# Moving a hybrid block's mixer stage off GpSimd arithmetic: conditioning to TensorE, weight splits and state-space products to VectorE

## The chip, the cores and the metric

The kernel runs on one core of a Trainium2 chip. The metric is device time in microseconds of one launch, the median of several runs. The engines are TensorE (PE; its weight loads are listed as PEld), VectorE (DVE), ScalarE (ACT), GpSimd (POOL) and SyncE (SP). SP, ACT and POOL also issue DMAs, each in a queue of its own that works in order with the engine's other instructions.

## What is computed

A sequence of 512 tokens of width 1024 goes through one conditioned block and two further layers. Cut to what matters here:

```python
def first_block(x, c, w_ada, b_ada, w_in, ...):
    ada = silu(c) @ w_ada[0] + b_ada[0]              # 6 * 1024 values
    sh_m, sc_m, g_m, sh_f, sc_f, g_f = split(ada, 6)
    h = rms_norm(x) * (1 + sc_m) + sh_m
    proj = h @ w_in[0]                               # 1792 columns z, 512 columns u
    z = z + mu * (z_prev - z)
    mix = concat([rwkv7_time_mix(z, ...), s5_mix(u, ...)]) @ w_out[0]
    x = x + g_m * mix
    h = rms_norm(x) * (1 + sc_f) + sh_f
    x = x + g_f * ((silu(h @ w_gate) * (h @ w_up)) @ w_down)
    return rms_norm(x) * final_gain
# then second_block: two layers of latent attention, short convolution and
# sliding-window attention, each x + concat(...) @ w_out_2
```

`ada` is one row of 6144 values. The first 2048 (shift and scale of the first norm) are needed before the first product, `g_m` before the mixer's output is added, the rest before the FFN.

## The kernel before

Activations lie feature-major: 128 features by 512 tokens a tile, eight tiles for x. Each f32 weight tile is loaded raw, copied by ACT to a rounded high part (`whi`), and the rest `wlo = wraw - whi` is taken by DVE or POOL. A product is then three matmuls of type fp32r: hi by hi, hi by lo, lo by hi. This splitting is in `Weights.convert` and, for the first product, in `conv0`. The engine of the subtraction is an entry of the weight list: for the mixer `LOENG` (POOL), for FFN and layers `LWENG` (DVE for every fourth tile, POOL for the others).

The program is a set of threads (Python generators) that yield instructions. The class `Flow` fixes one order for each engine before the program runs: at each turn it takes the instruction that can start first by a rough cost (`Flow.cost`) plus a bias of the thread (`BIAS`). Engines then run that order strictly, so an instruction whose input is late holds up whatever stands behind it on its engine. `turn` gives the weight products of the mixer (`gemm_g`) their places as filler between other matmuls.

The mixer (`mixer`, from L1497) has these parts, in the order of time:

- `norm_g` loads x, forms the norm and, feature tile by feature tile, `h`. Tile k needs the conditioning values k (shift) and 8 + k (scale).
- `cond` and `condpe` make these 16 groups of 128 values. The weights come transposed, so that for 12 of them one DVE instruction multiplies a 128x1024 tile `wa` by silu(c) spread over all partitions (`cact`) and sums along the row. For the four in `ADAPE`, `condpe` multiplies on PE with the weights stationary and one moving column. `loada0` loads the tiles on SP's queue into three buffers.
- `load0`, `conv0` and `gemm0` are the first product: u and three of the fourteen z blocks (`Z3 = (12, 0, 4)`), weights loaded on SP's queue, their low parts on POOL.
- `Prepare` builds the state-space matrices from their parameters on DVE; its `products` are eight items of five instructions, of which `PREP` gives four inject items and one output item to POOL and three output items to DVE. `response` clears the matrix `toep` on POOL and fills it by way of DRAM.
- `S5` is the state-space branch, from the first product's end to about 230 us.
- `Mix` is the time mix, four pairs of heads one after another (`front_a`, `invert`, `front_b`, `solve`, `chain`, `norm`), from about 180 to 500 us. Between its small matmuls PE does the remaining z blocks, the gate and the output products, in the order of `JOBS`; their weights are loaded on POOL's queue (`LOADQ`).
- `ada_g` makes the other 32 groups of conditioning values during the time mix: a tile `wa` is loaded on ACT's queue (`ADAQ`), multiplied by `cact` on POOL, and summed along the row by an ACT instruction with an accumulator. Two buffers.
- `evac_c` sums squares for the FFN's norm, two of its sums on POOL (`TAILENG`).

The FFN and the two layers follow (`second`), from about 490 us on; POOL has work of theirs too.

Of the kernel before, what the change touches and what calls it, by code (L numbers as in the profile page):

```python
# [8 lines left out]
F32 = mybir.dt.float32  # L9
# [16 lines left out]
# ---------------------------------------------------------------- host layout  # L26
# [71 lines left out]
LOENG = lambda X: X.pool  # L98
Z3 = (12, 0, 4)
# [44 lines left out]
def pack(i):  # L144
# [12 lines left out]
    o["w3"] = np.concatenate([w_in[:, 128 * m:128 * m + 128] for m in Z3], 1).reshape(8, 128, 3, 128)  # L157
# [60 lines left out]
# ---------------------------------------------------------------- device  # L218
class Ctx:
    """Engine shorthands and the helpers that every part uses."""  # L220
# [49 lines left out]
    def wtile(self, src, *shape, full=False):  # L270
        """weights as hi + lo, exactly"""
# [17 lines left out]
    def gemm(self, ps, src, K, hi, lo):  # L289
        """ps[128 cols, 512 tok] = sum_k src[:, k].T @ (hi + lo)[:, k]"""  # L290
# [10 lines left out]
    def gemms(self, pss, srcs, K, hi, lo, col, cols):  # L301
        """several products of the same operand, side by side; and of the column col, in parts, to cols"""
# [75 lines left out]
class Flow:  # L378
    """Puts the instructions of several threads (generators) in one order per engine: at each turn the
    instruction that can start first, by a rough count of what each takes, and keeps that order."""  # L380

    DMA_RATE = 360e3  # bytes a microsecond
    # from the end of an instruction on one engine to the start of one that needs it on another
# [10 lines left out]
    # -- an instruction: function, arguments; the first argument (or out) is written, the rest read  # L394
# [30 lines left out]
    def cost(eng, fn, out, args, kw=None):  # L425
# [4 lines left out]
        if eng == "PE":  # L430
# [11 lines left out]
            return 4 * max(n, m) / 2400.0  # L442
# [48 lines left out]
    # -- the tensor engine's clock: full speed only after a window with enough columns streamed  # L491
# [15 lines left out]
    def turn(self, o, plan, bias):  # L507
        """when this instruction would have its turn; work that fills in comes as the clock needs it"""
# [60 lines left out]
    def run(self):  # L569
        while self.live:  # L570
# [18 lines left out]
            # what is over before the best can start goes first  # L589
# [16 lines left out]
class Ring:  # L606
    """room for a few tiles of one kind, which threads take and free"""
# [22 lines left out]
class Pairs:  # L630
    """a ring of hi and lo"""
# [865 lines left out]
def mixer(X, top, stop):  # L1497
# [81 lines left out]
    def cond(cT):  # L1579
# [1321 lines left out]
```

## Time and profile before

| what | value |
|---|---|
| median of three runs | 1649.7 us (1642.33 to 1653.17) |
| profiled execution, first to last instruction | 1651.5 us |
| mean granted TensorE clock | 0.958 |
| busy PE / DVE / ACT / POOL | 1528.3 / 930.6 / 679.6 / 657.2 us |
| instructions PE / DVE / ACT / POOL | 8564 / 1988 / 1368 / 546 |
| moved by DMA | 141.88 MB |

The span of the profiled execution lies within the three runs and 1.8 us above their median; no other time of that execution is shown. Busy time is the union of an engine's instructions. A matmul's record lasts longer than its distance from the next one, so a busy PE can still take more. f32 matmuls have two records each. The granted clock is a share of 2.4 GHz.

### The profile page before, as it was taken

How to read it: one execution, taken by the hardware profiler on the slowest of the kernel's cores; microseconds unless marked ns; L12 is line 12 of the kernel's file. 1: busy time of each engine (PE TensorE's matmuls, PEld its weight loads, DVE VectorE, ACT ScalarE, POOL GpSimd, SP SyncE). 2: the span in 40 equal slices, each digit the busy share in tenths (PEclk: the TensorE clock that was granted, in tenths of full speed). 3: DMA queues.
4: the chain of work that ended last, by engine and by line, in shares of the span. 5: the costliest groups of instructions: out<-in, count | busy, mean ns of one | idle time of the engine just before them, and what ended most of it. 6: DMA issues, size and time to landing. Idle time of an engine off the chain costs nothing.

```text
span 1651.5 us, 23242 instructions
## 1 busy us (share of the span) xinstructions
PE 1528.3 (93%) x8564; PEld 1176.8 (71%) x8564; DVE 930.6 (56%) x1988; ACT 679.6 (41%) x1368; POOL 657.2 (40%) x546
## 2 busy tenths in 40 slices
PE   4699888798987999999999999999999999999998
PEld 4576575566655888888888867776778866867776
DVE  7986677867687422222215473464774575364772
ACT  3332443334434333333333465364454365355351
POOL 4652054555444333333443454632225344633222
PEclk9999997887998999999999999999999999999999
DMA  5453042453312222323332311312112311221112
GB/s 180 152 95 75 22 125 87 119 171 99 110 64 70 83 96 96 100 98 90 99 96 71 95 58 52 102 52 64 58 52 84 92 53 63 79 75 58 58 46 95
DMA packets 98800, 141.88 MB, mean 86 GB/s; under 512 B 40944, under 2 KB 45936, under 8 KB 98672
## 3 DMA queue, kind: packets, MB, share of 16 engines
q1 hardware_dynamic: 89360, 111.55, 22.9%
q10 hardware_dynamic: 5904, 17.85, 3.4%
q0 software_dynamic: 3424, 11.01, 2.2%
q8 instruction: 67, 1.10, 0.3%
q14 instruction: 45, 0.37, 0.1%
HBM read 135.39 MB, written 4.98 MB: 85 GB/s over the span
## 4 chain that ended last, share of the span: by engine, by line
PE 74%; DVE 20%; ACT 4%; issue 2%; DMA 0%; ACTq 0%; POOL 0%; DVEq 0%; POOLq 0%
PE mm L255 53%; PE rp L255 11%; PE O L255 3%; PE rp L524 3%; PE rq L255 2%; DVE wa L524 1%; PE cz L255 1%; DVE ca L236 1%; DVE rsy L252 1%; PE Y L255 1%; DVE sq L236 1%; DVE P L249 1%; DVE ctmp L236 1%; ACT qp L233 1%; DVE tm L236 1%
## 5 line engine op out<-in xcount | busy, mean ns | idle before, releaser
L236 POOL TENSOR_TENSOR wlo<-wraw,whi 128x512 fp32r<-128x512 f32 (+2 forms) x306 | 391.6, 1282 | 821.9 <-ACT whi L233 703.1
L233 ACT ACTIVATE whi<-wraw 128x512 fp32r<-128x512 f32 (+2 forms) x390 | 237.5, 613 | 425.1 <-PE mm L255 299.4
L255 PE MATMUL mm<-hhi,wlo 128*128 128x512 f32 x912 | 369.2, 405 | 3.2 <-DVE wlo L236 3.2
L255 PE MATMUL mm<-hhi,whi 128*128 128x512 f32 x912 | 367.2, 403 | 1.0 <-DVE ca L236 1.0
L255 PE MATMUL mm<-hlo,whi 128*128 128x512 f32 x912 | 365.4, 401 | 0.0
L255 PEld LDWEIGHTS mm<-hhi,wlo 128*128 128x128 f32 x912 | 175.4, 192 | 48.2 <-issue 6.6
L255 PEld LDWEIGHTS mm<-hhi,whi 128*128 128x128 f32 x912 | 175.0, 192 | 40.5 <-issue 5.8
L255 PEld LDWEIGHTS mm<-hlo,whi 128*128 128x128 f32 x912 | 174.7, 192 | 39.6 <-issue 4.1
L236 DVE TENSOR_TENSOR wlo<-wraw,whi 128x512 fp32r<-128x512 f32 (+1 forms) x84 | 67.1, 799 | 115.7 <-ACT whi L233 111.7
L255 PE MATMUL mm<-yhi,whi 128*128 128x512 f32 x224 | 92.1, 411 | 0.0
L255 PE MATMUL mm<-yhi,wlo 128*128 128x512 f32 x224 | 91.6, 409 | 0.0
L255 PE MATMUL mm<-ylo,whi 128*128 128x512 f32 x224 | 90.5, 404 | 0.0
L236 POOL TENSOR_TENSOR wa<-wa,cact 128x1024 f32<-128x1024 f32 x32 | 77.8, 2435 | 6.1 <-DMA wa<-in_wada 5.4
L255 PE MATMUL mm<-ahi,whi 128*128 128x512 f32 x176 | 69.3, 394 | 0.0
L255 PE MATMUL mm<-ahi,wlo 128*128 128x512 f32 x176 | 69.0, 392 | 0.0
L255 PE MATMUL mm<-alo,whi 128*128 128x512 f32 x176 | 68.3, 388 | 0.0
L236 DVE TENSOR_TENSOR xres<-xres,mm 128x512 f32<-128x512 f32 x48 | 32.9, 685 | 53.5 <-PE mm L255 53.4
L252 DVE SCALAR_TENSOR_TENSOR xres<-mm,ada,xres 128x512 f32<-128x512 f32 x40 | 29.5, 748 | 53.2 <-PE mm L255 53.1
L252 DVE SCALAR_TENSOR_TENSOR g<-th,mm 128x512 f32<-128x512 f32 x21 | 14.4, 688 | 71.6 <-PE mm L255 71.6
L252 DVE SCALAR_TENSOR_TENSOR th<-th,mm 128x512 f32<-128x512 f32 x20 | 13.7, 687 | 70.1 <-ACT th L233 70.1
L255 PEld LDWEIGHTS mm<-yhi,whi 128*128 128x128 f32 x224 | 43.0, 192 | 11.0 <-issue 1.8
L255 PEld LDWEIGHTS mm<-yhi,wlo 128*128 128x128 f32 x224 | 42.8, 191 | 11.1 <-issue 0.7
(550 smaller groups left out, 2935.4 us busy)
## 6 DMA issues: line engine op xcount, KB each, us to landing
wraw<-in_w2m SPq DMA_DIRECT2D x124, 256.0 KB, 2.7
wa<-in_wada ACTq DMA_DIRECT2D x32, 512.0 KB, 3.5
wraw<-in_wo SPq DMA_DIRECT2D x48, 256.0 KB, 2.6
wraw<-in_wgate SPq DMA_DIRECT2D x44, 256.0 KB, 2.6
wraw<-in_wup SPq DMA_DIRECT2D x44, 256.0 KB, 2.6
wraw<-in_wdown SPq DMA_DIRECT2D x40, 256.0 KB, 2.6
wa<-in_wada SPq DMA_DIRECT2D x16, 512.0 KB, 3.6
wraw<-in_wz POOLq DMA_DIRECT2D x22, 256.0 KB, 3.4
```

The costliest lines, as they stand in the source:

```text
L233: return self.act.activation(out=out, in_=in_, func=func, **kw)
L236: return (eng or self.dve).tensor_tensor(out=out, in0=a, in1=b, op=op)
L249: return self.dve.tensor_scalar(out=out, in0=a, scalar1=s1, scalar2=s2, op0=op0, **kw)
L252: return self.dve.scalar_tensor_tensor(out=out, in0=a, scalar=s, in1=b, op0=op0, op1=op1)
L255: return self.pe.matmul(out, lhsT=lhsT, rhs=rhs, start=start, stop=stop)
L524: ins = fn(*args, **kw)
```

## The change

Nothing in the mixer computes on POOL any more; what POOL keeps there are DMA issues and a few memsets.

1. First conditioning, `cond`: the weights come untransposed, 16 tiles of 128x1024 (`wss`). The moving operand is a 512-column half of a tile, the stationary one a column of silu(c) repeated 32 times; the eight products of a quarter go to four groups of 32 rows of one PSUM tile. ACT copies it out, four one-column products with `ones` add the rows up, and DVE adds the bias. A quarter gives shift and scale of two feature tiles. `condpe`, `cact` and the 12 DVE reductions go; four buffers instead of three.
2. Other conditioning, `ada_g`: eight one-column f32 products on PE for each of the 32 tiles, weights stationary, each into a PSUM column of its own; DVE sums them at the end of group 7 and of group 31. The loads become a thread of their own (`ada_load`) and move from ACT's queue to POOL's. The PSUM columns are half of the tile `cz`, which the time mix now allocates once instead of once per pair.
3. All weight splits of the mixer, those of `conv0` included, go from POOL to DVE. The first product's weight loads go from SP's queue to POOL's.
4. All eight items of `Prepare.products` and the clearing of `toep` are on DVE; so are the two sums of `evac_c`.
5. z block 0 leaves the first product and becomes the second job of `gemm_g`.
6. The planner's cost of an f32 matmul counts half the stationary columns.

```diff
-ADAQ = lambda nc: nc.scalar
+ADAQ = lambda nc: nc.gpsimd
-JOBS = [("z", m) for m in (13, 8)] + [("g", m) for m in range(4)] + ...
+JOBS = [("z", m) for m in (13, 0, 8)] + [("g", m) for m in range(4)] + ...
-NA0 = 3
-ADAPE = (0, 1, 2, 3)
-PREP = [0, 0, 0, 0, 1, 1, 1, 0]
-TAILENG = lambda X, m: X.pool if m in (3, 5) else X.dve
+NA0 = 4
+PREP = [1, 1, 1, 1, 1, 1, 1, 1]
-LOENG = lambda X: X.pool
-Z3 = (12, 0, 4)
+LOENG = lambda X: X.dve
+Z3 = (12, 4)
...
     def cost(eng, fn, out, args, kw=None):
-            return 4 * max(n, m) / 2400.0
+            return 4 * max(n, m / 2) / 2400.0
...
     def response(self):
-        yield o(X.pool.memset, self.toep, 0.0)
+        yield o(X.dve.memset, self.toep, 0.0)
...
     def cond(cT):
...
-        for i in range(16):
-            if i in ADAPE:
-                continue
-            yield lambda: st["la"] > i
-            wa, m = first.pop(("a", i)), i // 2 + 8 * (i % 2)
-            yield o(dve.tensor_tensor_reduce, out=wa, in0=wa, in1=cact, scale=1.0, scalar=V("bada", m),
-                    op0=ALU.mult, op1=ALU.add, accum_out=ada[:, m:m + 1])
+        res = X.mmt()
+        two = lambda a: a.rearrange("p (z k) -> p z k", z=2)
+        for j in range(4):
+            yield from X.take("yp", 1)
+            acc = X.yp.tile([128, 512], F32, name="yq", tag="Y")
+            for k in range(KD):
+                if k % 2 == 0:
+                    yield lambda: st["la"] > 4 * j + k // 2
+                    wa = first.pop(("a", 4 * j + k // 2))
+                q = slice(32 * (k % 4), 32 * (k % 4) + 32)
+                yield o(MM, acc[q], cT[:, k:k + 1].to_broadcast([128, 32]), wa[:, k % 2], k < 4, k > 3)
+                st["af"] |= {4 * j + k // 2} if k % 2 else set()
+            ev = xp.tile([128, 512], F32, name="ev", tag="ev")
+            yield o(ACT, ev, acc, scale=1.0 / 32.0)
+            X.give("yp", 1)
+            for c in range(4):
+                yield o(MM, res[:, 4 * j + c:4 * j + c + 1], ev[:, c * 128:(c + 1) * 128], C("ones"))
+            ks = slice(2 * j, 2 * j + 2)
+            yield o(X.ADD, two(ada[:, 0:16])[:, :, ks], two(res[:, 4 * j:4 * j + 4]), two(V("bada", 0, 16))[:, :, ks])
+            yield o(TS, oneplus[:, ks], ada[:, 8 + 2 * j:10 + 2 * j], 1.0, ALU.add)
...
     def load0():
-                yield o(nc.sync.dma_start, view(t), src)
+                yield o(LOADQ(nc).dma_start, view(t), src)
...
     def conv0():
-            yield from split_g(*hl, view(raw), X.dve if LO0[i] else X.pool)
+            yield from split_g(*hl, view(raw), X.dve)
...
     def ada_g():
-                yield o(MUL, w, w, cact, eng=pool)
-                yield o(ACT, w, w, accum_out=ada[:, 16 + i - NWA:17 + i - NWA])
+        ps = pools["ada"].rearrange("p (m k) -> p m k", k=KD)
+        for i in range(32):
+            yield lambda: ("a", 16 + i) in first
+            wa = first.pop(("a", 16 + i))
+            for k in range(KD):
+                yield o(MM, ps[:, i, k:k + 1], wa[:, k * 128:(k + 1) * 128], cT[:, k:k + 1])
+            st["ada"] += 1
+            if i in (7, 31):
+                c = slice(0, 8) if i == 7 else slice(8, 32)
+                a = slice(16 + c.start, 16 + c.stop)
+                yield o(dve.reduce_sum, out=ada[:, a], in_=ps[:, c], axis=AX.X)
...
```

## Rows read from the trace of the kernel before

**Rows 1.** Busy us (and count) of PE, PEld, DVE, ACT, POOL by stretch; PEclk, DMA share, GB/s.

```profile
8.00:116.00 108.00, 76.05 (x419) 66.84 (x420) 100.86 (x218) 35.86 (x67) 62.37 (x48) 0.95 0.43 136
116.00:232.00 116.00, 101.60 (x853) 73.88 (x853) 81.81 (x173) 42.03 (x75) 25.19 (x28) 0.94 0.32 59
232.00:500.00 268.00, 226.45 (x2060) 158.70 (x2054) 195.67 (x409) 100.77 (x185) 136.38 (x97) 0.88 0.38 112
...
533.00:880.00 347.00, 347.00 (x1509) 286.17 (x1510) 91.40 (x128) 117.03 (x195) 127.76 (x102) 0.99 0.31 95
```

**Rows 2.** The chain of waits from 8 to 116 us, shares by line.

```profile
by line: DVE wa L524 16.9%; DVE ctmp L236 10.3%; DVE ca L236 10.0%; PE rp L255 8.6%; DVE toep L236 8.2%; DVE x L236 6.6%; DVE hlo L236 4.9%; DVE sq L236 3.9%; PE mm L255 3.9%; DVE ph L252 3.6%; PE yq L255 3.1%; issue 2.3%; DVE pw L236 2.2%;
```

**Rows 3.** The same from 232 to 500 us: its longest piece (start, us, what).

```profile
295.00 6.72 DVE rsy L252
```

**Rows 4.** Timeline, 293 to 304 us: start, us, engine, line, operation, out<-in, form.

```profile
294.92 6.80 DVE L252 SCALAR_TENSOR_TENSOR rsy<-rsq,rsy 128x8 f32<-128x8 f32 x1
...
296.44 2.37 POOL L236 TENSOR_TENSOR wa<-wa,cact 128x1024 f32<-128x1024 f32 x1
...
299.34 2.35 POOL L236 TENSOR_TENSOR wa<-wa,cact 128x1024 f32<-128x1024 f32 x1
...
302.91 0.16 DVE L252 SCALAR_TENSOR_TENSOR rsy<-rsq,rsy 128x8 f32<-128x8 f32 x1
```

**Rows 5.** DVE groups by form, 8 to 116 us: count | busy us, mean ns | idle before.

```profile
L524 DVE CUSTOM_DVE_ANT_0 wa<-wa,cact,vecs 128x1024 f32<-128x1024 f32 x12 | 19.2, 1600 | 0.0
L236 DVE TENSOR_TENSOR toep<-s5c,pk 128x512 f32<-128x512 f32 x6 | 9.0, 1546 | 0.0
...
L236 DVE TENSOR_TENSOR ctmp<-ph 128x16 f32<-128x16 f32 x16 | 6.9, 468 | 0.1
...
L236 DVE TENSOR_TENSOR sq<-sq,ut 128x512 f32<-128x512 f32 x6 | 4.2, 692 | 0.5 <-ACT ut L233 0.3
...
L236 DVE TENSOR_TENSOR ctmp<-pw 128x16 f32<-128x16 f32 x4 | 2.4, 627 | 0.0
```

**Rows 6.** POOL groups by form, 116 to 500 us.

```profile
L236 POOL TENSOR_TENSOR wa<-wa,cact 128x1024 f32<-128x1024 f32 x32 | 77.8, 2435 | 6.1 <-DMA wa<-in_wada 5.4 <-PE rp L255 0.4
L236 POOL TENSOR_TENSOR wlo<-wraw,whi 128x512 fp32r<-128x512 f32 x39 | 52.5, 1347 | 182.6 <-ACT whi L233 110.6 <-issue 54.1 <-ACT UV L233 11.1
...
L236 POOL TENSOR_TENSOR wlo<-wraw,whi 128x256 fp32r<-128x256 f32 x8 | 5.8, 730 | 21.5 <-ACT whi L233 21.4
```

**Rows 7.** DVE groups by form, 232 to 500 us.

```profile
L252 DVE SCALAR_TENSOR_TENSOR rsy<-rsq,rsy 128x8 f32<-128x8 f32 x12 | 16.1, 1341 | 0.2
...
L236 DVE TENSOR_TENSOR tb<-tb,tm 64x24 f32<-64x24 f32 x6 | 5.2, 865 | 0.2
...
L236 DVE TENSOR_TENSOR KP<-w 128x512 f32<-128x512 f32 x3 | 4.8, 1611 | 0.0
...
L252 DVE SCALAR_TENSOR_TENSOR w<-w,k_kk 128x512 f32<-128x512 f32 x2 | 2.3, 1156 | 0.1
```

**Rows 8.** Timeline of PE at 31, 91 and 901 us.

```profile
31.55 3.58 PE L255 MATMUL yq<-cT,wa 128*128 128x1 f32 x16 [3.45 <-DVE ada L236]
...
91.81 0.40 PE L255 MATMUL mm<-hlo,w3hi 128*128 128x512 f32 x1
92.04 0.40 PE L255 MATMUL mm<-hhi,w3lo 128*128 128x512 f32 x1
...
93.64 2.02 PE L255 MATMUL yq<-ca,bbar 64*32 64x128 f32 x64
...
901.71 2.73 PE L255 MATMUL rp<-c,sq 128*128 128x1 f32 x24
```

**Rows 9.** PE group of full-width f32 products, 232 to 500 us.

```profile
L255 PE MATMUL rp<-rk,cr 128*128 128x512 f32 x6 | 3.7, 701 | 0.7 <-DVE rk L252 0.7
```

**Rows 10.** DMA issues on the page: KB each, median us to landing.

```profile
wraw<-in_wgate SPq DMA_DIRECT2D x44, 256.0 KB, 2.6
...
wraw<-in_wz POOLq DMA_DIRECT2D x22, 256.0 KB, 3.4
```

More of the change, by code (lines that the diff above doesn't have):

```diff
@@ L68 @@
 LOADQ = lambda nc: nc.gpsimd
-ADAQ = lambda nc: nc.scalar
+ADAQ = lambda nc: nc.gpsimd
 FILLMIN, FILLOFF = 3032, 0.6
-BIAS = {"s5": -3.13, "fronta": -0.3, "frontb": -0.1, "invert": 1.49, "solve": -1.12, "chain": -0.17, "norm": 0.2, "evac": 0.0, "glu": -0.2, "conv": -0.14, "ada": -0.07, "prep": -2.41, "w1p": -2.58, "wcp": -0.19, "wcd": 0.71, "toep": -0.79, "tw": 0.85, "x0": -2.96, "conv0": -1.87, "gemm0": 1.35, "loada0": -3.11, "load0": -1.83, "cond": -1.06, "condpe": -1.0, "late": 0.0, "fill": (-0.63, -1.38, 0.67, 0.88)}
-JOBS = [("z", m) for m in (13, 8)] + [("g", m) for m in range(4)] + [("z", m) for m in (5, 9, 1, 6, 2, 10, 11, 7, 3)]
+BIAS = {"s5": -3.13, "fronta": -0.3, "frontb": -0.1, "invert": 1.49, "solve": -1.12, "chain": -0.17, "norm": 0.2, "evac": 0.0, "glu": -0.2, "conv": -0.14, "ada": -0.07, "prep": -2.41, "w1p": -2.58, "wcp": -0.19, "wcd": 0.71, "toep": -0.79, "tw": 0.85, "x0": -2.96, "conv0": -1.87, "gemm0": 1.35, "loada0": -3.11, "load0": -1.83, "cond": -1.06, "loada": -1.0, "late": 0.0, "fill": (-0.63, -1.38, 0.67, 0.88)}
+JOBS = [("z", m) for m in (13, 0, 8)] + [("g", m) for m in range(4)] + [("z", m) for m in (5, 9, 1, 6, 2, 10, 11, 7, 3)]
 JOBS += [(k, m) for k in "xabc" for m in range(8)]
-LO0 = [0] * 16
-NA0 = 3
+NA0 = 4
 SLACK = 0.05
 PHASE = 0.0
-ADAPE = (0, 1, 2, 3)
-PREP = [0, 0, 0, 0, 1, 1, 1, 0]
+PREP = [1, 1, 1, 1, 1, 1, 1, 1]
 HENG = [0, 1, 0, 1, 0, 1, 0, 1]
-TAILENG = lambda X, m: X.pool if m in (3, 5) else X.dve
 QENG = lambda X: X.dve
@@ L1528, in mixer @@
     flow = X.flow
-    st = dict(raw=0, conv=0, used=0, gemm=0, evac=0, ada=0, zz=0, ms=0, z=0, x=0, c1=0, sin=0, ca=0, w1=0, tw=0, toep=0, w=set(), c=set(), ad=set(), summed=0, xs=0, kind="", adas=0,
+    st = dict(raw=0, conv=0, used=0, gemm=0, evac=0, ada=0, zz=0, ms=0, z=0, x=0, c1=0, sin=0, ca=0, w1=0, tw=0, toep=0, w=set(), c=set(), adk=0, summed=0, xs=0, kind="", adas=0,
               af=set(), ct=0, l0=0, w0=0, h0=0, k0=0, began=0, la=0, cact=0)
@@ L1548, in norm_g @@
         flow.spawn(cond(cT), BIAS["cond"])
-        flow.spawn(condpe(cT), BIAS["condpe"])
         flow.spawn(prep.discretise(), BIAS["prep"])
@@ L1602, in condpe @@
-    def condpe(cT):
-        yield lambda: st["ct"]
-        yield from X.take("yp", 1)
-        ps = X.yp.tile([128, 512], F32, name="yq", tag="Y")
-        for i in ADAPE:
-            yield lambda: st["la"] > i
-            wa, m = first.pop(("a", i)), i // 2 + 8 * (i % 2)
-            for k in range(KD):
-                yield o(MM, ps[:, m:m + 1], wa[:, k * 128:(k + 1) * 128], cT[:, k:k + 1], k == 0, k == KD - 1)
-            st["af"].add(i)
-            yield o(X.ADD, ada[:, m:m + 1], ps[:, m:m + 1], V("bada", m))
-            st["ad"].add(i)
-        X.give("yp", 1)
+        yield o(TS, omu, V("mu", 0, 14), -1.0, ALU.mult, 1.0, ALU.add)
@@ L1638, in conv0 @@
             if i % 2:
-                hl = [xp.tile([128, 3, 128], F32R, name=n, tag=n, bufs=2) for n in ("w3hi", "w3lo")]
+                hl = [xp.tile([128, len(Z3), 128], F32R, name=n, tag=n, bufs=2) for n in ("w3hi", "w3lo")]
             else:
@@ L1650, in gemm0 @@
         yield lambda: st["h0"] > 0 and st["w0"] > 0
-        up, zps = [X.rpt() for _ in range(4)], [X.mmt() for _ in range(3)]
+        up, zps = [X.rpt() for _ in range(4)], [X.mmt() for _ in Z3]
         for k in range(KD):
@@ L1659, in gemm0 @@
                 yield o(MM, up[j], hhi[:, k, j::4], wu[1], False, p_)
-            for i in range(3):
+            for i in range(len(Z3)):
                 yield o(MM, zps[i], wz[0][:, i], hhi[:, k], s_, False)
@@ L1668, in gemm0 @@
                     up[j].rearrange("p (g c) -> p g c", c=16))
-        st["evac"] = -3
+        st["evac"] = -len(Z3)
         for i, m in enumerate(Z3):
-            yield from evac_z(i - 3, m, zps[i])
+            yield from evac_z(i - len(Z3), m, zps[i])
         xst.close()
@@ L1793, in load_x @@
             st["x"] += 2
[L1794 to L1795 removed]
+        yield lambda: st["adas"] > 0
         st["x"] += 1
@@ L1879, in finish @@
     def finish():
-        yield lambda: st["summed"] > KD and st["adas"]
+        yield lambda: st["summed"] > KD and st["adas"] > 1
         if stop in ("h", "s5", "rwkv", "x1"):
```

65 lines of the change are left out of this document (29 added, 36 removed).

## Prediction

> **What bounds the kernel now.** I read the busy times by stretch first, then the chain that ended last in the two stretches that the change touches, then the groups of VectorE (DVE) and GpSimd (POOL) there, then single instructions in order of time. The stretches [rows 1] show three different limits. From 533 to 880 us PE is busy for all of 347 us; that is the FFN, and neither it nor the two layers behind it are touched by the change. From 8 to 116 us, the first norm, the conditioning and the first product, DVE is busy for 100.9 of 108 us and PE for 76.1: DVE is the bound, and its share of the chain says the same [rows 2], with the conditioning product `wa` first at 16.9%. From 232 to 500 us, the time mix, PE is busy for 226.5 of 268 us at a granted clock of 0.88 and DVE for 195.7; the chain goes to and fro between the two, and its longest piece, 6.72 us at 295.00, is on DVE [rows 3].
>
> Why DVE is slow there is in the timeline [rows 4]. The instruction that writes `rsy`, 128x8, takes 6.80 us at 294.92, and the same form 0.16 us at 302.91. POOL had two sums running (296.44 for 2.37 and 299.34 for 2.35), and the DVE instruction ends at 301.72, POOL's second at 301.69. So a DVE instruction with two inputs in SBUF that meets a running POOL tensor instruction stands still until POOL is done. That is the price of arithmetic on POOL that no busy time of POOL shows.
>
> **The change part by part.** Stretch 8 to 116 us, on DVE, which bounds it:
> - The 12 conditioning reductions go: 19.2 us [rows 5].
> - POOL runs no arithmetic any more, so the others fall to what they take alone. 128x512 alone is 0.69 us (`sq<-sq,ut`), 128x16 0.17. Eleven groups from `toep<-s5c,pk` (6 x (1.546 - 0.69) = 5.1) by way of `ctmp<-ph` (16 x (0.468 - 0.17) = 4.8) to `ctmp<-pw` (4 x (0.627 - 0.17) = 1.8) give 26.5 us [rows 5]. The smaller groups I leave out.
> - The state-space products that POOL did come over: PREP has five such items of five instructions, four items of 448 columns and one of 512, so 20 x 0.60 + 5 x 0.69 = 15.5 us.
> - The splits of the first product's weights: 8 x 0.69 + 8 x 0.35 (256 columns, by proportion) = 8.3 us.
> - The memset of `toep`, 4096 columns: no DVE row has one of this size; at the rate of the 128x512 row it takes 5.5 us, and below it could be as short as one such instruction, 0.7. I take 3.
>
> Sum: -19.2 - 26.5 + 15.5 + 8.3 + 3 = -18.9 us. DVE stays the bound, so the stage gives **-19**; if the smaller groups count too it is more, and PE is next.
>
> On PE in that stretch, the four tiles of `condpe` go and 32 products of 512 columns come, f32 with 32 stationary columns, in four column groups. Each is two records. The nearest row of such narrow products side by side has 64 records of 128 columns in 2.02 us [rows 8], 0.03 each, so 64 records of four times the width take 8 us. One after the other, at the 3.7 / 6 = 0.62 us of a full-width f32 record of 512 columns [rows 9], they take 40. I take 8, since the kernel's own narrow products do run side by side. PE has 32 us idle there to hide it; at 40 us the idle time is used up, and with DVE's work shrinking the stage's gain is gone. The 24 products of feature block 0 leave this stretch and come back later as filler.
>
> The loads: 16 conditioning tiles stay on SP, with four buffers for three; 16 weight loads go from SP to POOL's queue, and 32 later conditioning loads from ACT's queue to POOL's. A load on POOL's queue lands 3.4 us after issue, one on SP's 2.6 [rows 10]; 0.8 each, which buffers of two to four tiles hide, so nothing in the sum, at worst 48 x 0.8 = 38 us.
>
> A rule weighed here: the Trainium skill, page "SBUF — State Buffer", section "SBUF: two separate sides", says that a DMA issued from GpSimd's queue starves while a VectorE copy or scalar instruction in a two-port mode runs, 620 ns becoming some 3100. It speaks against moving loads to that queue; 48 times that difference would be an estimate of 119 us of queue time. In this trace the queue's loads already run beside a DVE that is busy for most of the stage and are late by 0.8 us, so I go by the row.
>
> Stretch 232 to 500 us. POOL's 32 products `wa` (77.8 us) and ACT's sums behind them go, with the 47 splits (52.5 + 5.8 us) [rows 6]. The splits come to DVE: 39 x 0.69 + 8 x 0.35 = 30 us, over this stretch and the one before. DVE loses its standing still: eighteen groups from `rsy` (12 x (1.341 - 0.166) = 14.1), with `tb` (6 x (0.865 - 0.18) = 4.1) and `KP` (3 x (1.611 - 0.69) = 2.8), to `w<-w,k_kk` (2 x (1.156 - 0.69) = 0.9), sum to 46.5 us [rows 7]. DVE was 73% busy and gets no worse, and its part of the chain could shrink by up to 46.5.
>
> Against that, PE gets 32 x 8 one-column f32 products with 128x128 weights, two records each: 512 records. At full clock 24 such records take 2.73 us, 0.112 each [rows 8], so 57 us; at 31.55 us 16 take 3.58, 0.22 each, as at the 1.2 GHz level, so 114 us. The planner counts each product as half of the 0.22 us that it takes, and block 0's 24 products (about 0.235 apart, 5.6 us) come here or just before. PE's idle time is 41.6 us, but that is just the time in which it waited for DVE, so it shrinks as DVE gets faster. What is late next is PE: 226.5 + 57 + 5.6 = 289. The clock is 0.88 of 2.4 GHz on average, hence a quarter of the stretch at the lower level; where PE is busy throughout it is 0.99 [rows 1]. If the added products close the gaps, some 28 us of PE's time come back (226.5 x 0.12), which leaves 261. I take 263 with a little idle time: **-5**, with -47 (all of DVE's gain, products hidden) and +78 (114 us at the low level, 41.6 hidden, 5.6 added) as ends.
>
> Stretch 116 to 232: PE 101.6 busy of 116 [rows 1], some of DVE's splits come here, and DVE has a third of it idle: 0. From 500 us on: 0.
>
> Sum: -19 - 5 = -24 on a span of 1651.5 us gives 1627.5. The span stands 1.8 us above the median of the three runs, 1649.7, and within them, so the median should be **1626**.
>
> **The rivals.**
> - B, PE takes back what DVE gives: the clock in the time mix stays at 0.88, the stretch becomes 289 us (+21). 1651.5 - 19 + 21 - 1.8 = 1652: no change. For: 41.6 us of idle time against 63 of new work. Against: PE's records are 0.40 us long and 0.23 apart [rows 8], so a PE that counts as busy still has room.
> - C, DVE's queue stands at the splits: slower. On POOL the 47 splits waited 110.6 + 21.4 us for ACT's copy `whi` [rows 6], 2.8 us each, and nobody stood behind them. On DVE, which works in order, everything of the time mix stands behind. If 1.1 us of the 2.8 falls on the chain, it is 52 us: 1678. It decides from 24 / 47 = 0.51 us a split. Against: the planner puts a split where it expects its input.
> - D, the one-column products cost the chain nothing: PE keeps pace with a faster DVE, and of the 46.5 us some 28 show: 1651.5 - 19 - 28 - 1.8 = 1603. For: as above, records overlap. The Trainium skill, page "TensorEngine Tiling (Array Packing)", section "Performance Considerations", says that a product with one column has the latency of one with sixty; worked out from its figures that is an estimate of 13 us for the 512 records and would lead to D, too. Against: the row at 901.71 has 0.112 a record, over four times that.
> - E, the loads on POOL's queue come late and nothing hides it: 1626 + 38 = 1664.
>
> **How the numbers follow.** Forecast 0.57, B 0.13, C 0.15, D 0.12, E 0.03. Two runs can be told apart here at about 1%, so below 1633 is faster and above 1666 slower. The forecast's own range is 1605 to 1645, and a fifth of it lies above 1633: faster 0.46 + 0.12 (D) = 0.58; same 0.11 + 0.13 + 0.03 = 0.27; slower 0.15. The range for 8 in 10 has to leave out most of C and the far half of D: 1585 to 1668.
>
> **What would show it.** Right: no TENSOR_TENSOR on POOL before 480 us; `rsy` 128x8 never over 0.4 us there; the first product's last record some 20 us earlier; a granted clock above 0.9 in the time mix and PE idle under 25 us of it; 512 records of `cT,wa` with a spacing near 0.11. Wrong: the conditioning's 512-column records one after the other (8 us becomes 30 or more); PE's wait on the DVE splits `wlo` in the chain (C); the time mix no shorter than 280 us (B); loads landing later than 4 us and ACT's `whi` waiting for them (E). If the stretch from 533 us on differs by over 1% of itself, the planner's new order has moved work that I left at nothing.

## The result, and the profile after

| | us |
|---|---|
| before, median of 4 runs beside the changed kernel | 1646.0 |
| after, median of 4 runs (1685.7 to 1725.6) | 1713.0 |
| ratio, 95% interval | 1.0286 (1.0229 to 1.0344) |
| after, profiled execution: its time / its span | 1703.7 / 1702.0 |
| forecast, range | 1626, 1585 to 1668 |

The change makes the kernel slower, and the time lies above the range. The comparison leaves the two longest runs out (1722.2 and 1725.6), so this ratio rests on two; six more runs of the same kernel (after_again, below), from 1712.5 to 1727.1, gave 1719.2 and 1.0436 (1.0406 to 1.0467).

The stretches of the profile after, with the columns of [rows 1]:

```profile
8.00:80.00 72.00, 59.96 (x288) 44.86 (x288) 60.99 (x191) 35.47 (x68) 9.10 (x17) 1.00 0.53 187
80.00:200.00 120.00, 105.14 (x967) 77.24 (x966) 93.88 (x227) 43.78 (x78) 6.99 (x13) 0.96 0.33 64
200.00:510.00 310.00, 302.64 (x2496) 238.18 (x2495) 140.79 (x388) 53.88 (x96) 29.67 (x57) 0.77 0.31 89
...
550.00:930.00 380.00, 376.31 (x1663) 307.40 (x1664) 116.13 (x166) 130.65 (x218) 142.36 (x112) 0.98 0.31 93
```

Up to 200 us the kernel is ahead, in the time mix (here 200 to 550 us) it loses more than it had won, and the FFN and the layers only stand 47 to 51 us later. What [rows 1] showed as a stretch bounded by DVE (8 to 116 us) now ends at about 80 us. What it showed as a time mix with PE 226.5 of 268 us busy at a clock of 0.88 now has PE busy for 302.6 of 310 us, at 0.77. DVE, 195.7 of 268 us before, is busy for 140.8 of 310.

The table that the rest of this text uses: where the last product of the gated unit starts (the end of the state-space stage), where the first FFN product starts (the end of the time mix), the difference, and within it the time in which PE was idle and the granted clock, each from one profiled execution. The prediction's stretch from 232 to 500 us lies within the 294.5 us of the kernel before.

| kernel | state space ends | FFN starts | time mix | PE idle in it | its clock |
|---|---|---|---|---|---|
| before | 208.7 | 503.2 | 294.5 | 46.9 | 0.88 |
| after | 178.8 | 550.5 | 371.7 | 20.7 | 0.80 |
| after_again | 201.1 | 569.4 | 368.3 | 20.4 | 0.80 |
| cols64 | 180.4 | 502.1 | 321.7 | 21.2 | 0.96 |
| dose1 | 178.9 | 452.8 | 273.9 | 29.6 | 0.95 |
| ada_pool | 178.7 | 490.4 | 311.7 | 53.4 | 0.87 |
| first_only | 185.5 | 488.4 | 302.9 | 52.1 | 0.88 |
| ada_dve | 179.6 | 484.5 | 304.9 | 56.5 | 0.85 |
| lo_pool | 186.7 | 567.2 | 380.5 | 20.2 | 0.76 |
| before_onecol | 206.9 | 591.3 | 384.4 | 31.1 | 0.77 |
| before_cols64 | 207.2 | 551.8 | 344.6 | 30.3 | 0.89 |
| moving | 202.0 | 502.9 | 300.9 | 23.4 | 0.97 |
| half | 204.2 | 521.1 | 316.9 | 38.3 | 0.90 |
| dve_lift | 177.1 | 487.1 | 310.0 | 59.8 | 0.85 |

So the first stages gave 30 us in this profile, and the time mix took 77.

Who holds the time mix up is in the chain of waits from 200 to 510 us:

```profile
by line: PE cz L252 30.7%; PE mm L252 28.9%; PE rq L252 12.2%; PE rp L252 10.5%; PE Y L252 6.9%; PE rp L521 3.7%; issue 2.4%; DVE Z L249 0.9%; PE rq L521 0.7%; DVE tb L521 0.5%; DVE UV L233 0.5%; DVE wlo L233 0.4%; ACT UV L230 0.3%; DVE tm 
```

Nearly all of it is PE; before, it went to and fro between PE and DVE. The first name, `cz`, holds the new one-column products and those of the serial chain over the chunks, which share that bank. The waits of the same stretch (who waits for whom, us in total, times, longest):

```profile
POOL wa L521 <- PE cz L252: 179.2, 29, 14.0
...
DVE Z L249 <- PE cz L252: 30.3, 25, 3.1
DVE UV L233 <- PE cz L252: 28.7, 19, 3.7
...
DVE wlo L233 <- ACT whi L230: 20.8, 8, 5.7
```

POOL's 179 us are loads that wait for a buffer; no load on POOL's queue is among the names that the chain shows. DVE's instructions of the serial chain (`Z`, `UV`) wait for PE; in-order PE has one-column products ahead of the product that they need. DVE's splits wait for ACT's copy 20.8 us in total, and make 0.4% of the chain.

PE's groups by form, and two places of its timeline:

```profile
L252 PE MATMUL cz<-cT,wa 128*128 128x1 f32 x512 | 86.5, 282 | 5.4 <-DVE Z L249 2.9 <-DVE UV L233 1.9 <-DVE Z L521 0.6
L252 PE MATMUL mm<-hhi,whi 128*128 128x512 f32 x56 | 32.1, 574 | 0.0
```

```profile
255.04 1.87 PE L252 MATMUL cz<-cT,wa 128*128 128x1 f32 x8 [0.39 <-DVE UV L233]
...
272.52 2.22 PE L252 MATMUL cz<-cT,wa 128*128 128x1 f32 x16
```

The one-column records are 0.23 us apart at 255 us (8 in 1.87 us, granted clock 0.50) and 0.14 at 272 us (16 in 2.22, granted clock 0.78 from 272 to 275); [rows 8] had 0.22 and 0.11. And the 512-column products beside them, `mm<-hhi,whi`, take 574 ns in the mean, where the same form took 439 before.

The contention of DVE with POOL went as forecast. DVE from 200 to 510 us:

```profile
L233 DVE TENSOR_TENSOR wlo<-wraw,whi 128x512 fp32r<-128x512 f32 x22 | 15.1, 687 | 21.6 <-ACT whi L230 20.2 <-issue 0.9 <-PE mm L252 0.4
...
L233 DVE TENSOR_TENSOR KP<-w 128x512 f32<-128x512 f32 x3 | 2.0, 682 | 0.0
L249 DVE SCALAR_TENSOR_TENSOR rsy<-rsq,rsy 128x8 f32<-128x8 f32 x9 | 1.5, 167 | 0.3
...
L233 DVE TENSOR_TENSOR tb<-tb,tm 64x24 f32<-64x24 f32 x6 | 1.1, 180 | 0.2
```

Against [rows 7], `rsy` falls from 1341 to 167 ns, `KP` from 1611 to 682, `tb` from 865 to 180. From 8 to 80 us, DVE and then PE's narrow products side by side:

```profile
L233 DVE TENSOR_TENSOR toep<-s5c,pk 128x512 f32<-128x512 f32 x8 | 5.3, 684 | 0.0
L233 DVE TENSOR_TENSOR toep<-bbar,pk 128x448 f32<-128x448 f32 x8 | 4.6, 618 | 0.0
...
L233 DVE TENSOR_TENSOR ctmp<-ph 128x16 f32<-128x16 f32 x8 | 1.2, 170 | 0.1
```

```profile
L252 PE MATMUL yq<-wa,cT 128*32 128x512 f32 x64 | 13.9, 716 | 1.6 <-DMA wa<-in_wss 1.6
```

Against [rows 5], `toep<-s5c,pk` falls from 1546 to 684 ns and `ctmp<-ph` from 468 to 170. The loads on POOL's queue land after 3.0 to 4.3 us; the last two of these lines are the first product's, which took 3.2 and 2.4 us on SP's queue before:

```profile
wa<-in_wada POOLq DMA_DIRECT2D x32, 512.0 KB, 3.7
...
wraw<-in_wz POOLq DMA_DIRECT2D x24, 256.0 KB, 3.0
...
wraw<-in_wu POOLq DMA_DIRECT2D x8, 256.0 KB, 4.3
...
wraw<-in_w POOLq DMA_DIRECT2D x8, 128.0 KB, 4.0
```

### The profile page after: what moved, and what is told of

Its sections match the earlier page's. It is cut to its first block, busy times and chain, and to the rows that moved or that the text cites. A ratio compares the mean times of both kernels' runs of the same rounds, so it can differ in the third digit from the quotient of the medians.

```text
span 1702.0 us, 24235 instructions
## 1 busy us (share of the span) xinstructions
PE 1616.7 (95%) x9092; PEld 1254.2 (74%) x9092; DVE 881.3 (52%) x2054; ACT 648.3 (38%) x1308; POOL 488.4 (29%) x474
## 4 chain that ended last, share of the span: by engine, by line
PE 82%; DVE 12%; ACT 3%; issue 2%; DMA 1%; ACTq 0%; SPq 0%; POOL 0%; DVEq 0%
PE mm L252 53%; PE rp L252 13%; PE cz L252 6%; PE rp L521 3%; PE O L252 3%; PE rq L252 2%; PE Y L252 1%; DVE P L246 1%; DVE wlo L233 1%; DVE sq L233 1%; ACT qp L230 1%; DVE xres L249 1%; ACT sq L230 1%; DVE qp L249 1%; PE yq L252 1%
## 5 line engine op out<-in xcount | busy, mean ns | idle before, releaser
L233 POOL TENSOR_TENSOR wlo<-wraw,whi 128x512 fp32r<-128x512 f32 (+2 forms) x252 | 322.1, 1280 | 595.2 <-ACT whi L230 551.1
L252 PE MATMUL mm<-hhi,wlo 128*128 128x512 f32 x920 | 374.1, 407 | 4.3 <-DVE wlo L233 4.2
L252 PE MATMUL mm<-hhi,whi 128*128 128x512 f32 x920 | 375.7, 408 | 1.0 <-DVE ca L233 1.0
L252 PE MATMUL mm<-hlo,whi 128*128 128x512 f32 x920 | 371.3, 404 | 0.0
L233 DVE TENSOR_TENSOR wlo<-wraw,whi 128x512 fp32r<-128x512 f32 (+2 forms) x140 | 100.9, 721 | 146.7 <-ACT whi L230 144.7
L252 PEld LDWEIGHTS cz<-cT,wa 128*128 128x128 f32 x512 | 85.8, 239 | 15.7 <-DVE Z L249 3.8
L252 PE MATMUL cz<-cT,wa 128*128 128x1 f32 x512 | 86.5, 282 | 5.4 <-DVE Z L249 2.9
L521 POOL DMA_DIRECT2D wa<-in_wada x32 | 16.9, 530 | 181.2 <-PE cz L252 179.2
```

Of the source, the lines that this page charges most:

```text
L233: return (eng or self.dve).tensor_tensor(out=out, in0=a, in1=b, op=op)
L252: return self.pe.matmul(out, lhsT=lhsT, rhs=rhs, start=start, stop=stop)
L521: ins = fn(*args, **kw)
```

## The experiments

Three theories stood after this comparison. CLOCK: one-column products keep PE busy without lifting its clock, and everything beside them then runs at the lower of the two levels (1.2 GHz). QUEUE: they are simply long, in an engine that works in order, and the clock is a bystander. SPLITS: another part of the change (the splits on DVE, the queues) holds the time mix up. The diffs below are shortened to the calls that differ. Only cols64 (against after), before_cols64 (against before_onecol) and after_again keep the order of every engine's instructions; in the other variants the planner lays the order out anew, so their differences hold that too.

**cols64: more columns, the same order.** The order of every engine's instructions is that of the changed kernel.

```diff
-pools["ada"] = cz[:, 256:512]
+pools["ada"] = cz[:, 192:512]
-MM(ps[:, i, k:k + 1], wa[:, k * 128:(k + 1) * 128], cT[:, k:k + 1])
+MM(pw[:, 8 * i + k:8 * i + k + 64], wa[:, k * 128:(k + 1) * 128], cT[:, k:k + 1].to_broadcast([128, 64]))
```

> The changed kernel with one thing altered: each of the 256 late conditioning products streams 64 columns (the same column 64 times) where it streamed one; only the first is used. Weight tiles, number of products and the order of every engine's instructions are those of the changed kernel. Theory CLOCK (one-column products occupy TensorE without lifting its clock, and everything beside them runs at the lower level): the granted clock of the time mix (0.77 after the change) rises above 0.9, the 302.6 us of TensorE work in that stretch shrink to some 240, and the kernel ends at 1640 to 1665 us although more columns are streamed. Rival QUEUE (the products are simply 57 to 87 us of records in an engine that works in order; the clock is a bystander): the time does not fall, 1700 to 1730. Rival SPLITS (weight splits on VectorE or the queues of the loads are what costs): 1695 to 1710, nothing changes.

Measured: 1677.0 us (1655.3 to 1679.6), ratio 1.0151 (1.0081 to 1.0220). Its time mix, its PE groups, and one place of its timeline:

```profile
200.00:510.00 310.00, 291.05 (x2659) 223.35 (x2660) 182.78 (x474) 73.86 (x131) 38.63 (x68) 0.96 0.35 102
```

```profile
L252 PE MATMUL cz<-cT,wa 128*128 128x64 f32 x512 | 74.9, 280 | 5.4 <-DVE Z L249 2.9 <-DVE UV L233 1.9 <-DVE Z L521 0.6
L252 PE MATMUL mm<-hhi,whi 128*128 128x512 f32 x56 | 25.8, 461 | 0.0
```

```profile
260.40 1.89 PE L252 MATMUL cz<-cT,wa 128*128 128x64 f32 x16
```

PE streams 64 times the columns in these products and is done earlier: the granted clock goes from 0.77 to 0.96, 512-column products from 574 to 461 ns, the records themselves from 86.5 us to 74.9 (16 in 1.89 us, 0.12 apart), the time mix from 371.7 to 321.7 us. PE was busy for the same share of the time mix in both, 351.0 of 371.7 us and 300.5 of 321.7. Beside the columns only their place in the PSUM bank differs, so 50 us of the time mix in these two profiles were the clock; between the medians lie 36 (42 to after_again). CLOCK's time of 1640 to 1665 was missed by 12 us, and the 240 us of PE work were not reached: the records' own time stays. QUEUE is true as well, for the rest.

**after_again: the changed kernel once more,** beside before_cols64 and dve_lift below, with no edit.

> The changed kernel itself, unaltered, beside the two that follow: its time had 4 runs from 1686 to 1726. All theories: 1685 to 1726 us, a ratio of 1.02 to 1.05. CLOCK names the price of the one-column products' clock as what lies between this and cols64 (1677 us, ratio 1.015): 20 to 40 us.

Measured: 1719.2 us (1712.5 to 1727.1), as expected. Its time mix, 368.3 us, is that of the first profile; its state space ends 22 us later, for which see the last section.

**before_onecol and before_cols64: the same two on the kernel before.** Only the late conditioning goes to one-column products, with its loads on POOL's queue and the planner's new cost; then these get 64 columns.

```diff
-yield o(MUL, w, w, cact, eng=pool)
-yield o(ACT, w, w, accum_out=ada[:, 16 + i - NWA:17 + i - NWA])
+for k in range(KD):
+    yield o(MM, ps[:, i, k:k + 1], wa[:, k * 128:(k + 1) * 128], cT[:, k:k + 1])
```

> The kernel before with only the late conditioning changed: one-column products on TensorE, loads through GpSimd's queue, the planner's new cost for such products. First conditioning, splits and state-space products as before. CLOCK: the granted clock from 232 us to the end of the time mix falls from 0.88 to below 0.8 and the kernel ends at 1700 to 1735. QUEUE: the granted clock stays at 0.85 or more, TensorE's busy time there rises by 57 to 87 us, of which its idle 28 us hide a part: 1680 to 1710. SPLITS: 1640 to 1660.

> The kernel before_onecol with 64 columns streamed by each late conditioning product, in the same order: the test of cols64 on the other kernel. CLOCK: the granted clock of the time mix rises from 0.74 to above 0.9 and the end falls from 1745 by 30 to 60 us, to 1685 to 1715. QUEUE: no fall, 1740 to 1770.

Measured: 1745.0 us, ratio 1.0558 (1.0499 to 1.0618), and 1706.1 us, ratio 1.0343 (1.0306 to 1.0379). Their time mixes, one column and then 64:

```profile
232.00:590.00 358.00, 329.74 (x2515) 255.84 (x2512) 161.35 (x406) 66.66 (x118) 74.17 (x94) 0.76 0.29 85
```

```profile
232.00:551.00 319.00, 291.55 (x2530) 223.55 (x2530) 162.55 (x408) 67.13 (x120) 74.53 (x95) 0.89 0.33 96
```

This one edit, alone, costs the kernel before 99 us, more than the whole change and 10 more than CLOCK's range allowed. At 64 columns it costs 59: the clock goes from 0.76 to 0.89 and the time mix from 384.4 to 344.6 us. So the clock's price is seen a second time, 40 us, in another kernel and with other work around it; the expected 0.9 was just missed.

**dose1: an eighth of the products.** The others are left out, so the late conditioning's values are not whole.

```diff
-for k in range(KD):
+for k in range(1):
     yield o(MM, ps[:, i, k:k + 1], wa[:, k * 128:(k + 1) * 128], cT[:, k:k + 1])
```

> The changed kernel with 32 of the 256 late one-column products left (one of the eight of each weight tile; the others are left out, so the modulation values are not whole; the loads and all else stay). It is the floor of the time mix without these products. The changed kernel stands at 1713, cols64 at 1677. QUEUE and CLOCK together: with 7/8 of 86.5 us of records gone the end falls to 1605 to 1635, the granted clock of the time mix is 0.85 to 0.95; what cols64 lies above this is the records' own time at the upper clock level (some 40 to 60 us), and what the changed kernel lies above cols64 is the clock. If something else of the change held the time mix up, the end stays above 1660.

Measured: 1611.3 us (1601.2 to 1619.6), ratio 0.9799 (0.9759 to 0.9838). Its time mix:

```profile
200.00:453.00 253.00, 226.29 (x2157) 161.75 (x2157) 174.50 (x454) 70.82 (x127) 37.65 (x67) 0.94 0.42 122
```

With the one-column products nearly gone the kernel is 35 us below before, and SPLITS falls as the cause of the loss. The 35 us are no price of the rest of the change, since the work of the late conditioning is left out here and not done elsewhere. From dose1 to cols64, with about the same clock in both (0.95 and 0.96), the time mix grows from 273.9 to 321.7 us: 47.8 us for 448 records, 0.107 each. That is nearly all of their 0.12 us, so little of it is hidden. Extended to all 512 records it is 54.6 us.

**ada_pool and first_only: parts undone.** In ada_pool the late conditioning is POOL's and ACT's again; in first_only the time mix's splits too are POOL's.

```diff
-MM(ps[:, i, k:k + 1], wa[:, k * 128:(k + 1) * 128], cT[:, k:k + 1])
+MUL(w, w, cact, eng=pool); ACT(w, w, accum_out=ada[:, 16 + i - NWA:17 + i - NWA])
...
-LOENG = lambda X: X.dve
+LOENG = lambda X: X.pool
```

> The changed kernel with the late conditioning (the last 32 weight tiles) put back as before: multiplied by the broadcast silu(c) on GpSimd, summed on ScalarE, loaded through ScalarE's queue. The broadcast tile is built at the time mix's start. All the rest of the change stays: the first conditioning on TensorE, splits and state-space products on VectorE. CLOCK and QUEUE both: the 30 us that the changed kernel had gained by the end of the state-space stage stay, and the time mix takes what it took before: 1610 to 1630 us, granted clock of the time mix at 0.85 or more. SPLITS: the time mix stays long, 1680 to 1705.

> The kernel ada_pool with the time mix's weight splits moved back to GpSimd too: of the change only the part up to the end of the state-space stage is left (first conditioning on TensorE, first splits, squares and Toeplitz products off GpSimd), and the time mix is that of before. It prices that part by itself. If the 30 us by which the changed kernel was ahead at the end of the state-space products carry to the end: 1612 to 1625 us. If the time mix gives them back whatever stands in it: 1640 to 1655. SPLITS (the splits on VectorE were what ada_pool lost by): at least 15 us below ada_pool's 1653.

Measured: ada_pool 1653.2 us (1633.7 to 1662.5), ratio 0.9976 (0.9936 to 1.0016), no difference from before; first_only 1635.8 us (1629.4 to 1646.0), ratio 0.9929 (0.9902 to 0.9956). Without the one-column products the loss is gone, as CLOCK and QUEUE had it, but neither kernel reaches what was expected of it: first_only lies between its two ranges, and ada_pool does not come down to 1630: its time mix is 311.7 us, not 294.5. POOL's multiplications are back and now meet the splits on DVE too. DVE of ada_pool, 200 to 510 us:

```profile
L233 DVE TENSOR_TENSOR wlo<-wraw,whi 128x512 fp32r<-128x512 f32 x28 | 21.6, 772 | 3.1 <-ACT whi L230 2.2 <-PE mm L252 0.5
...
L233 DVE TENSOR_TENSOR KP<-w 128x512 f32<-128x512 f32 x3 | 6.9, 2287 | 0.0
...
L249 DVE SCALAR_TENSOR_TENSOR rsy<-rsq,rsy 128x8 f32<-128x8 f32 x12 | 4.4, 368 | 0.3
```

`KP` is at 2287 ns (682 in the changed kernel) and `rsy` at 368. With the splits on POOL again (first_only) the time mix is 302.9 us; its 8 us above before hold the 24 products of feature block 0, moved here from the first product, which the prediction had at 5.6. SPLITS had asked for 15 us between the two kernels and got 17 by the medians, 9 by the time mix: true of the two together with POOL's multiplications, and small. The part of the change up to the end of the state space is worth 23 us there (208.7 to 185.5), of which 12 reach the end by the medians.

**lo_pool: the splits back on POOL, the one-column products kept.**

```diff
-LOENG = lambda X: X.dve
+LOENG = lambda X: X.pool
```

> The changed kernel with the time mix's weight splits back on GpSimd; the one-column products stay. CLOCK and QUEUE: no gain, 1695 to 1725, granted clock of the time mix below 0.82. SPLITS: 20 us or more below the changed kernel, 1660 to 1690.

Measured: 1726.7 us, ratio 1.0489 (1.0443 to 1.0535); clock 0.76, time mix 380.5 us. No gain, and 2 us more than expected: against SPLITS once more.

**moving, ada_dve, half and dve_lift: other places for the late conditioning.** First with the weights as the moving operand:

```diff
-MM(ps[:, i, k:k + 1], wa[:, k * 128:(k + 1) * 128], cT[:, k:k + 1])
+MM(acc[32 * k:32 * k + 32], cT[:, kk:kk + 1].to_broadcast([128, 32]), wa[:, k])   # 256 columns
+ACT(ev, acc, scale=1.0 / 32.0)
+MM(res[:, n:n + 1], ev[:, c * 128:(c + 1) * 128], C("ones"))
```

> The changed kernel with the late conditioning in the form of the first: the weights are the moving operand (128 products of 256 columns, four side by side on 32 output rows each), evacuated by ScalarE and summed over the rows by 64 one-column products. CLOCK: granted clock of the time mix above 0.85, some 20 to 30 us of TensorE's time for these products in place of 86.5, end at 1610 to 1640 us. QUEUE: TensorE's time falls by 55 to 65 us and the end with it, 1640 to 1650, with a granted clock still near 0.77. SPLITS: 1680 to 1705.

Measured: 1652.7 us (1631.2 to 1662.3), ratio 0.9993 (0.9949 to 1.0037). The clock of the time mix is 0.97 and 60 us are back, so that QUEUE's clock near 0.77 falls, but the median missed 1640. Its time mix, 300.9 us, is 71 us below after's and 6 above before's; 23 us of what is missing lie ahead of it, in a state-space stage that ran at the lower level in this profile (202.0 against 178.8, see the last section). The two fastest runs, 1631.2 and 1631.7, are inside CLOCK's range. The products, 200 to 510 us:

```profile
L253 PE MATMUL cz<-wa,cT 128*32 128x256 f32 x256 | 32.3, 398 | 3.3 <-DVE Z L522 1.5 <-DVE Z L250 1.4 <-DVE UV L234 0.5
...
L253 PE MATMUL cz<-c,eva 128*128 128x1 f32 x128 | 19.4, 247 | 2.7 <-DVE UV L234 1.7 <-DVE Z L250 0.7 <-DVE Z L522 0.4
```

The two groups take 51.7 us where 20 to 30 were expected: the sums by one-column products cost 0.15 us a record.

On DVE:

```diff
-MM(ps[:, i, k:k + 1], wa[:, k * 128:(k + 1) * 128], cT[:, k:k + 1])
+dve.tensor_tensor_reduce(out=w, in0=w, in1=cact, scale=1.0, scalar=V("bada", m), op0=ALU.mult, op1=ALU.add, accum_out=ada[:, m:m + 1])
```

> The changed kernel with the late conditioning on VectorE (32 products with their sums in one instruction each, loads through GpSimd's queue); no one-column products, and GpSimd still without arithmetic until the time mix's end. CLOCK and QUEUE: TensorE's 86.5 us of one-column records are gone, its stretch from 200 us to the time mix's end shrinks to 255 to 270 us, and the end falls to 1605 to 1630. SPLITS, or a VectorE that becomes the bound with some 40 us more: 1640 to 1670, with TensorE waiting for VectorE in the stretch.

Measured: 1647.6 us in the median of 12 runs (1624.4 to 1657.1), where the kernel before had 1648.0 beside it. Its reductions, and the two halves of its time mix:

```profile
L521 DVE CUSTOM_DVE_ANT_0 wa<-wa,cact,vecs 128x1024 f32<-128x1024 f32 x32 | 40.9, 1278 | 0.4
```

```profile
200.00:350.00 150.00, 139.83 (x1434) 102.08 (x1430) 123.01 (x289) 41.99 (x75) 29.34 (x56) 0.97 0.56 168
350.00:505.00 155.00, 111.55 (x804) 80.89 (x803) 104.38 (x255) 38.60 (x67) 15.91 (x17) 0.74 0.16 47
```

The one instruction of each tile takes 1278 ns with no arithmetic on POOL beside it (1600 in [rows 5]). But the gain does not arrive: the work that fills PE's gaps is, but for the last output products, used up by 350 us, and then PE is idle for 43 of 155 us at a clock of 0.74. The median is that of the second expectation; PE's waits there are mostly for DVE. The next kernel tries to fill that half.

```diff
+if i < 16: dve.tensor_tensor_reduce(...)      # the first 16 tiles
+else: MM(pw[:, n:n + 64], wa[:, k * 128:(k + 1) * 128], cT[:, k:k + 1].to_broadcast([128, 64]))
```

> The changed kernel with the late conditioning halved: the first 16 weight tiles on VectorE (one instruction each), the last 16 as products of 64 columns on TensorE, late in the time mix, where ada_dve left TensorE idle for 43 of 155 us at a granted clock of 0.74. If TensorE's idle time there is open to them and they lift the clock, 35 us of records cost little: 1605 to 1625 us, granted clock above 0.9 to the time mix's end. If they only stand in TensorE's queue: 1640 to 1665.

Measured: 1676.1 us, ratio 1.0171 (1.0148 to 1.0195): worse than either expectation, but 25 us of it lie ahead of the time mix: in its profile the state-space stage ran at the lower level and ended at 204.2 us (179.6 in ada_dve). The time mix is 12 us longer than ada_dve's. The products came from 320 to 428 us, ahead of the time mix's own work in PE's queue, and from 470 to 520 us PE was busy for 29.4 of 50 us at a clock of 0.74.

```diff
+for k in range(12):
+    MM(lift, hhi[:, k % 8, 0:128], hhi[:, k % 8])
 for hf in range(2):
...
     ps = yield from y(hf, q)
```

> The kernel ada_dve with twelve idle products of 512 columns put ahead of the state-space stage's output products (their result is not used). In two profiles with the same order of TensorE's work these output products ran at a granted clock of 1.00 in one (31 us) and of 0.50 in the other (53 us), the second after a pause of 1.6 us at their start; and ada_dve's runs fell into 1624 to 1632 and 1647 to 1657 us. If the clock at which that stage is entered decides it, nearly all runs lie at 1622 to 1636 us; if not, they still fall into two groups some 23 us apart.

Measured: 1640.7 us in the median; eight of nine runs at 1634.0 to 1647.5, and one at 2431.8 with a granted clock of 0.55 over its whole span; ratio 0.9962 (0.9936 to 0.9989). The state-space products run at 1.00, and the time mix's second half idles as in ada_dve:

```profile
110.00:150.00 40.00, 39.94 (x231) 25.42 (x232) 24.52 (x42) 7.33 (x13) 1.07 (x2) 1.00 0.09 25
350.00:480.00 130.00, 91.43 (x705) 65.18 (x704) 85.08 (x224) 25.19 (x45) 6.21 (x10) 0.71 0.16 44
```

The two groups of runs are gone, but the whole lies some 10 us above the faster one of ada_dve: inconclusive as to the gain.

Of the versions that compute the whole, the lowest median is first_only's, 0.7% below before; ada_dve has the lower best run (1624.4) and no lower median than before.

## Why the prediction was wrong

**The step that failed** is "if the added products close the gaps, some 28 us of PE's time come back", which made 289 us into 261 and the time mix into -5. The gaps were in large part closed, PE was busy for 302.6 of 310 us, and the clock fell from 0.88 to 0.77 there (0.80 over the whole time mix). The profile's busy share is not what the clock goes by: at 94% busy it was 0.80 with one column a record, at 93% it was 0.96 with 64. The records of one column keep PE busy and the clock low, and the lower level covers the other products between them, too. By cols64 and before_cols64 that is 40 to 50 us.

The prediction used the two rows of such records [rows 8] as a price for the records alone. The trace of before had a sign of the rest behind the second of them, the 24 records from 901.71 us on. PE is busy throughout, and yet:

```profile
900.00:905.00 5.00, 5.00 (x36) 4.61 (x35) 2.85 (x9) 3.22 (x7) 0.96 (x1) 1.00 0.12 31
905.00:910.00 5.00, 5.00 (x17) 3.93 (x16) 4.21 (x29) 0.00 (x0) 0.00 (x0) 0.66 0.00 0
```

```profile
904.85 0.39 PE L255 MATMUL mm<-hhi,wlo 128*128 128x512 f32 x1
...
906.25 0.63 PE L255 MATMUL mm<-hhi,whi 128*128 128x512 f32 x1
```

It is a sign and no proof: in first_only the clock does not fall behind the same 24 records. The row at 31.55 us says less than the prediction read in it: beside its spacing, which is that of the lower level, the profile shows a granted clock of 1.00 for 31.50 to 35.20 us, and PE had been idle for 3.45 us before it. The level there is not settled.

The terms of the time mix, from the table: 371.7 - 294.5 = +77.

| term | forecast | measured |
|---|---|---|
| the records at the upper level | +57 | +55 (dose1 to cols64, extended to all) |
| block 0's products, all that DVE gives, and a clock that comes back as the gaps close | -62 (-34 and -28) | -27 (dose1 less its own eighth: 273.9 - 6.8 - 294.5) |
| a clock that the records pull down | 0 | +50 (after against cols64) |

The price of a record, 0.112 us, was right. The clock does come back where the records are few or wide (0.95 in dose1, 0.96 in cols64), but with one column it goes the other way, and that is 50 of the 82 us between forecast and measurement. Another 35 are a gain that was forecast too large: of PE's idle time the sum left 2 us, and the runs left 29.6 of 46.9 in dose1, 21.2 in cols64 and 20.7 in after. Of the 27 us, 17 are idle time; the other 10 are what the clock gave back less block 0's products, which no run prices apart.

The upper end of the forecast's sum, +78, meets the measured +77 by chance. It had all records at the lower level, 114 us, and all idle time used up; the records took 86.5 us, PE's idle time fell by 26, and the rest is the other products at the lower level. It was named as a bound, cut from the range, and given to no rival.

Of the signs of being right that were named, `rsy` stayed at 166 to 169 ns in all twelve places, and PE was idle for under 25 us; a clock above 0.9 and a spacing near 0.11 did not come. The two POOL instructions that the prediction calls sums [rows 4] are the multiplications by `cact`.

**The stretch from 8 to 116 us** was right in mechanism and too small: ACT's first copy of the first product starts at 76.7 us where it started at 113.3, -36.6 for a forecast of -19. The smaller groups that were left out, and block 0's 24 products that left this stretch, are in the difference; they were not priced apart. The narrow products took 13.9 us (forecast 8, 40 if serial), and the stage came out shorter than forecast all the same; later in the stretch 16 of their records took 1.92 us, 0.12 each, the forecast's price. Of the 36.6 us, 30 are left at the end of the state space.

**Rivals.** B had the right place, with a clock that stays at 0.88; the clock fell, and the time mix lost over three times B's 21 us. C: the splits wait 20.8 us for ACT in all, 0.4% of the chain; lo_pool and dose1 exclude it. D: the records cost 0.107 us each, nearly none of it hidden. "TensorEngine Tiling (Array Packing)" of the Trainium skill, section "Performance Considerations", had led there; that one column takes as long as sixty agrees with these runs (0.11 us a record with one column, 0.12 with 64), but the 13 us estimated from its overhead do not hold for these f32 products with 128 stationary columns, which took 55. E: the loads landed 3.0 to 4.3 us after issue, so that one part of its sign came, but ACT waited for one of them only, for 1.4 us; elsewhere the loads waited for buffers.

**From 500 us on** nothing changed, as forecast: from the FFN's first product to the first layer's first output product it is 433 and 434 us (503.2 to 936.3, 550.5 to 984.1).

## What to carry to other kernels

TensorE's busy share did not tell its clock here: before work is put into its gaps, look for a row of just that kind of work, read at which level it ran, and then how long the work behind it took. A matrix-vector product with the weights stationary took as long with one column as with 64, and with one column it held the clock down for the work between; widening the moving operand, at no use to the result, is a cheap test that leaves the order alone. And a bound that was worked out and then cut from the range should first be asked which mechanism would reach it.

## What was not expected of the hardware

The same instructions can settle at either clock level. In the profiles of after and of after_again, one kernel, the state-space stage's output products follow one another without a gap (120 to 145 us):

```profile
120.00:145.00 25.00, 25.00 (x158) 15.71 (x158) 12.87 (x22) 4.20 (x7) 1.07 (x2) 1.00 0.07 22
```

```profile
120.00:145.00 25.00, 25.00 (x90) 14.78 (x89) 11.07 (x19) 2.97 (x5) 1.08 (x2) 0.50 0.07 22
```

PE counts as busy for all 25.00 us in both, at 1.00 in one and 0.50 in the other, and gets through 158 records or 90. A pause just before is 0.86 us long in the first and 1.14 in the second:

```profile
115.43 0.43 PE L252 MATMUL rp<-ca,sr 64*64 64x128 f32 x2 [0.86 <-DVE sr L233]
...
118.97 0.65 PE L252 MATMUL rp<-ca,sr 64*64 64x128 f32 x4
119.55 0.43 PE L252 MATMUL rp<-toep,ug 128*64 128x128 f32 x2
```

```profile
115.43 0.43 PE L252 MATMUL rp<-ca,sr 64*64 64x128 f32 x2 [1.14 <-DVE sr L233]
...
119.48 1.11 PE L252 MATMUL rp<-ca,sr 64*64 64x128 f32 x4
120.52 0.69 PE L252 MATMUL rp<-toep,ug 128*64 128x128 f32 x2
```

Four records take 0.65 us in the one and 1.11 in the other, and it stays so to the stage's end: 31 us against 52 (113.8 to 144.8, 113.5 to 165.1). That is why the same kernel's first stages are ahead by 30 us in one profile and by 8 in the other, and it fits the spread of ada_dve's runs; the kernel before was at 1.00 in this stage in its profile.

The length of the pause does not decide it. In moving and half the pause was 1.62 and 1.54 us and the stage ran at 0.50, as one would think from the two above; but in cols64 and ada_dve it was longer than in after_again, and the stage ran at 1.00:

```profile
117.06 0.43 PE L252 MATMUL rp<-ca,sr 64*64 64x128 f32 x2 [1.15 <-DVE sr L233]
```

```profile
116.17 0.43 PE L252 MATMUL rp<-ca,sr 64*64 64x128 f32 x2 [1.17 <-DVE sr L233]
```

dve_lift, with twelve wide products ahead of the stage, had no such pause and 1.00 there, in the one execution that was profiled. What decides stays open.

The Trainium skill, page "TensorE: Matmul & The Clock Gate", section "Part 1: The HAM clock gate", sets the level by how busy PE has been. Here, as in the time mix, a PE that the profile counts as busy throughout stayed at the lower one; by the profile's count of busy time the rule does not hold, and no run shows what count the chip itself goes by.
